# FFN accumulators in single PSUM banks, and the first pair's silu chain a few products later

## The chip, the cores and the metric

The kernel runs on one core of a Trainium2 chip. The metric is device time in microseconds of one launch; the time before is the median of three runs. One further execution was taken with the hardware profiler; its rows are what the prediction works with. Engines in those rows: PE (TensorE matmuls), PEld (TensorE weight loads), DVE (VectorE), ACT (ScalarE), POOL (GpSimd), SP (SyncE, which issues the DMAs).

## What is computed

One step of a two-layer streaming encoder over 640 rows (512 frames of a new stream, and 8 running streams of 16 frames) with a width of 1024, in fp32. Each layer is an FFN, a mixer, and another FFN; a last RMSNorm follows.

```python
for l in range(DEPTH):      # DEPTH = 2
    x = x + 0.5 * swiglu(rmsnorm(x, norm_g[l, 0]), ffn_w_gate[l, 0], ffn_w_up[l, 0], ffn_w_down[l, 0])
    hn = rmsnorm(x, norm_g[l, 1])
    out = mixer_ab(hn, ...) if l % 2 == 0 else mixer_c(hn, ...)
    x = x + out
    x = x + 0.5 * swiglu(rmsnorm(x, norm_g[l, 2]), ffn_w_gate[l, 1], ffn_w_up[l, 1], ffn_w_down[l, 1])

def swiglu(x, w_gate, w_up, w_down):
    return (jax.nn.silu(x @ w_gate) * (x @ w_up)) @ w_down
```

The inner width of an FFN is 2816. The mixers (mLSTM and SSD heads in layer 0, gated DeltaNet in layer 1) are untouched by the change except for the PSUM pool that they draw from.

## The kernel before

Activations lie transposed: eight tiles x of 128 features by 640 tokens. The stages run in order: FFN 0a, mixer ab, FFN 0b, FFN 1a, mixer gdn, FFN 1b; the last FFN ends in finish (L2065), which also writes the output. Every fp32 factor is split into a high and a low part, and each product is three matmul passes (high by high, high by low, low by high).

**PSUM.** A partition has eight banks of 512 fp32. One pool, opened in the constructor (L60), serves the whole program: big (L123) gives a tile of two banks, with two buffers, and small (L127) one bank, with four. The 640 tokens take two halves of 320 (HT), each in a bank of its own. A tile that is asked for when its tag's buffers are taken waits for the oldest one's readers.

**An FFN** (L653) works on 22 blocks of 128 inner columns, in eleven pairs, and builds one list of jobs that pipe (L589) issues. For each job: its matmuls, then sums for later weights on DVE, then the job's post (evictions), then the splits of weights that have become possible. in_order (L638) chains what a job issues to what the job before it issued on the same engine, so that PE, DVE, ACT and POOL each take the jobs in the order of the list.

- *Weights.* A unit of weights is split on ACT (high, L617) and POOL (low, L618) into two of eight buffers wsp, so a unit is split four units ahead, when the job of the unit four back is done. Raw weights come by DMAs of 1 MB (wload, L174).
- *The first pair* (first_jobs, L496) is done by plain products, since it runs while the block operands are still being made. Loop jobs 0 to 3 accumulate the gate's four sums (two big tiles) and half of up (q, two small), then rstd_cols (L359, one small); two jobs do the other half of up (v, two small), then rstd_rows (L372, into one big), which makes R, the per-token factor. end (L543) multiplies the gate by R, takes its silu on ACT, multiplies q and v by R out of PSUM, makes the last block operands (next(blocks): four L315 on ACT, four L316 on DVE) and the hidden activations (hidden, L478: L481 on DVE, L483 on ACT, L486 on DVE). loop_end (L521) copies the gate sums out of PSUM on ACT (L526) and makes the other block operands (blocks2, L309).
- *The other ten pairs* (pair_jobs, L430) use a scheme of seven block products in place of eight. The jobs of a pair are g4 (gate products 0 to 3), u4 (up 0 to 3), g3 (gate 4 to 6), u3 (up 4 to 6), each of twelve matmuls, then four down tiles of the group before. Product 0 to 3 open banks 0 to 3; products 4, 5 and 6 accumulate on banks 0, 2 and 3. The posts add the banks into an SBUF tile: product 0 is copied on ACT (p1, L456), the others are added on DVE (L452), and p4 ends with the gate's silu (L469). The gate's four banks are two big tiles, and up's four are small:

```python
if whole:
    x, y = self.big(), self.big()
    bank.update(enumerate((x[:, 0, :HT], x[:, 1, :HT], y[:, 0, :HT], y[:, 1, :HT])))
else:
    bank.update(enumerate(self.small()[:, :HT] for _ in range(4)))
```

- *Down* (down_jobs, L556): two of four down tiles are big and evicted by one DVE instruction, two are pairs of small and evicted by two (L580). In the first of the pair's groups a down tile has two blocks to sum over (12 matmuls), later four (24).
- *setup* (L146) for the coming mixer is called behind the first of the ten pairs in FFN 0a and 1a; its conv_setup (L904) takes three or six small tiles (L917) for short transposes, outside in_order.

At a stage's end each down tile is followed by prep (L298), which makes the next stage's operand xg from x. Each stage opens an SBUF pool of its own (section, L113) and closes it at its end.

Of the kernel before, what the change touches and what calls it, by code (L numbers as in the profile page):

```python
# [8 lines left out]
F32 = mybir.dt.float32  # L9
# [7 lines left out]
P = 128  # L17
T = 640
# [35 lines left out]
class Trunk:  # L54
    def __init__(self, ctx, tc, io):
# [3 lines left out]
        self.dram = ctx.enter_context(tc.tile_pool(name="dram", bufs=2, space=bass.MemoryType.DRAM))  # L59
        self.ps = ctx.enter_context(tc.tile_pool(name="ps", bufs=1, space=PSUM))  # L60
        self.n = 0
# [57 lines left out]
    def ext(self, which, dtype=F32):  # L119

        return lambda tag, shape, bufs=1: self.t(f"ext{which}", shape, {"A": 6, "B": 4, "C": 2}[which], dtype)

    def big(self):  # L123
        self.n += 1
        return self.ps.tile([P, 2, 512], F32, tag="big", name=f"big_{self.n}", bufs=2)

    def small(self):  # L127
        self.n += 1
        return self.ps.tile([P, 512], F32, tag="small", name=f"small_{self.n}", bufs=4)

# [299 lines left out]
    def pair_jobs(self, tile, raw, whole):  # L430
# [5 lines left out]
        def run(i, b, first, last):  # L436
            def go():
                if i == 0:
                    if whole:
                        x, y = self.big(), self.big()  # L440
                        bank.update(enumerate((x[:, 0, :HT], x[:, 1, :HT], y[:, 0, :HT], y[:, 1, :HT])))
                    else:
                        bank.update(enumerate(self.small()[:, :HT] for _ in range(4)))
                self.block_product(bank[b], w[i], [x[i] for x in self.xs], first, last)

            return go
# [49 lines left out]
    def first_jobs(self, tile, raw_g, raw_u, which, h):  # L496

        nc = self.nc
        blocks = self.blocks2(tile, which)
        G = [Unit(lambda m=m: raw_g.v[:, 2 * m : 2 * m + 2], None, raw_g if m == 3 else None, 2) for m in range(4)]  # L500
        Q, V = (
            [Unit(lambda m=m, c=c: raw_u.v[:, 4 * m : 4 * m + 4, c : c + P], None, raw_u if c and m else None) for m in range(2)] for c in (0, P)
        )
        ps, res = {}, {}

        def loop(m):
            def go():
                if m == 0:
                    ps["g"] = [self.big() for _ in range(2)]
                    ps["q"] = [self.small()[:, :HT] for _ in range(2)]  # L510
                for k in (2 * m, 2 * m + 1):
                    for c, t in enumerate(ps["g"]):
                        w = [part[:, k % 2, c * P : c * P + P] for part in G[m].parts]
                        self.half_passes([t[:, i, :HT] for i in range(2)], w, self.xg[k], k == 0, k == ND - 1)
                    self.half_passes(ps["q"], [part[:, k % 4] for part in Q[m // 2].parts], self.xg[k], k == 0, k == ND - 1)
                if m == 3:
                    self.rstd_cols()

            return go

        def loop_end(m):  # L521
            def go():
                if m == 3:
                    g, _ = res["g"], res["u"] = [tile("h", [P, 2 * T], bufs=8) for _ in range(2)]
                    for i, t in enumerate(ps["g"]):
                        nc.scalar.copy(g[:, i * T : i * T + T].rearrange("p (a b) -> p a b", a=2), t[:, :, :HT])  # L526
                next(blocks)

            return go

        def second(m):
            def go():
                if m == 0:
                    ps["v"] = [self.small()[:, :HT] for _ in range(2)]
                for k in range(4 * m, 4 * m + 4):
                    self.half_passes(ps["v"], [part[:, k % 4] for part in V[m].parts], self.xg[k], k == 0, k == ND - 1)
                if m == 1:
                    t = self.big()
                    self.rstd_rows(t[:, 0], t[:, 1])

            return go

        def end():  # L543
            g, u = res["g"], res["u"]
            for i in range(2):
                nc.vector.tensor_tensor(g[:, i * T : i * T + T], g[:, i * T : i * T + T], self.R, ALU.mult)
            nc.scalar.activation(out=g, in_=g, func=AF.Silu)
            for i, t in enumerate(ps["q"] + ps["v"]):
                nc.vector.tensor_tensor(u[:, i * HT : i * HT + HT], t, self.R[:, i % 2 * HT : i % 2 * HT + HT], ALU.mult)
            next(blocks)  # L550
            list(self.hidden(tile, g, u, h))

        jobs = [Job([G[m], Q[m // 2]], loop(m), loop_end(m)) for m in range(4)]
        return jobs + [Job([V[0]], second(0)), Job([V[1]], second(1), end)]

    def down_jobs(self, raw, h, j0, nxt):  # L556
# [6 lines left out]
        def job(j, c):  # L563
            unit, at, out, ps = units[c // b], c % b, [], []

            def run():
                if j % 4 < 2:
                    t = self.big()
                    ps.append(t[:, :, :HT])
                    out.extend(t[:, i, :HT] for i in range(2))  # L570
                else:
                    out.extend(self.small()[:, :HT] for _ in range(2))
                    ps.extend(out)
                for k in range(n):
                    self.half_passes(out, [part[:, k, at : at + P] for part in unit.parts], h[k], k == 0, k == n - 1)

            def post():
                x = self.x[j].rearrange("p (a b) -> p a b", a=2)
                for dst, src in [(x, ps[0])] if len(ps) == 1 else [(x[:, i], ps[i]) for i in range(2)]:
                    nc.vector.scalar_tensor_tensor(dst, src, 0.5, dst, ALU.mult, ALU.add)  # L580
                if nxt is not None:
                    nxt(j)
# [70 lines left out]
    def ffn(self, tile, l, s, nxt, mid):  # L653
# [23 lines left out]
        hs = [[] for _ in FF_GROUPS]  # L677
        jobs = self.first_jobs(tile, gates[0], ups[0], 3 * l + 2 * s, hs[0])
        for g, (g0, g1) in enumerate(FF_GROUPS):
            for f in range(max(g0, 2), g1, 2):  # L680
# [14 lines left out]
                u3[2].post = lambda post=u3[2].post, begin=begin: begin(post)  # L695
                down[0].post = lambda post=down[0].post, rest=rest: rest(post)
                jobs += g4 + u4 + g3 + u3 + down
                if f == 2 and mid is not None:
# [1366 lines left out]
    def finish(self, tile, w, acts):  # L2065
# [4 lines left out]
        for ts in (range(0, 3), range(3, NT)):  # L2070
# [48 lines left out]
    def run(self, stages):  # L2119
# [5 lines left out]

        self.load_x(0, 0, after(0))
        if stages[0][0] != "ffn":
            self.setup(stages[0][0])
# [57 lines left out]
```

## Time and profile before

| | us |
|---|---|
| median of three runs | 3109.37 |
| lowest, highest | 3107.22, 3112.12 |
| profiled execution | 3101.83 |
| its span, first to last instruction | 3100.1 |

| engine | busy us | share |
|---|---|---|
| PE | 2908.4 | 94% |
| PEld | 2766.8 | 89% |
| DVE | 1867.9 | 60% |
| POOL | 1459.7 | 47% |
| ACT | 1253.6 | 40% |

A row of the groups by shape reads: line, engine, operation, out<-in by the program's names, shapes, count, then busy us and mean ns of one, then the idle time of the engine just before those instructions and what ended it. A row of the timeline reads: start and length in us, engine, line, operation, out<-in, shapes, how many were merged, and in brackets the idle time before it and what ended that. big and small are the PSUM tags. Times are counted from the span's start. Where a wait is for several things, the view names the one that came last.

### The profile page before, as it was taken

What the parts mean: (1) busy time and instruction counts of PE and PEld (TensorE: products, weight loads), DVE (VectorE), ACT (ScalarE), POOL (GpSimd) and SP (SyncE); (2) the same over time, 40 slices, a digit from 0 to 9 for tenths busy, and PEclk for the clock granted to TensorE, in tenths of its full rate; (3) what the DMA queues carried; (4) which work ended last, traced back from release to release, by engine and by line L of the source; (5) the groups of instructions that cost most, each with busy time, mean ns of one, the idle gap of its engine ahead of it and who ended that gap; (6) DMA issues with size and microseconds to landing.
All of it is one profiled execution on the core that took longest, in us unless ns stands there. A gap on an engine that the chain in (4) does not pass through costs nothing. (4 is left out here: it accounts for less than half of the span.)

```text
span 3100.1 us, 51054 instructions
## 1 busy us (share of the span) xinstructions
PE 2908.4 (94%) x19910; PEld 2766.8 (89%) x19910; DVE 1867.9 (60%) x3455; ACT 1253.6 (40%) x2647; POOL 1459.7 (47%) x1039
## 2 busy tenths in 40 slices
PE   6999999999999998999998999999999998899998
PEld 6899999888889887999997999998888898899998
DVE  6565556323566676665655655556777756566665
ACT  5333334333344344333343333344565454333335
POOL 3666663222223125666644666653323222566664
PEclk8999999999999999999998999999999999999999
DMA  3222222222212221222221222221222212122222
GB/s 100 75 82 82 69 69 83 71 81 89 91 57 88 74 82 49 85 71 82 82 70 58 82 80 71 82 69 56 57 72 59 82 54 86 59 84 70 69 82 89
DMA packets 245159, 232.13 MB, mean 75 GB/s; under 512 B 22135, under 2 KB 221956, under 8 KB 244918
## 3 DMA queue, kind: packets, MB, share of 16 engines
q1 hardware_dynamic: 244918, 228.87, 23.9%
q8 instruction: 157, 2.57, 0.3%
q14 instruction: 84, 0.69, 0.1%
HBM read 210.23 MB, written 18.60 MB: 74 GB/s over the span
## 5 line engine op out<-in xcount | busy, mean ns | idle before, releaser
L618 POOL TENSOR_TENSOR wsp<-wraw,wsp 128x512 fp32r<-128x512 f32 x600 | 886.0, 1486 | 708.2 <-ACT wsp L617 679.8
L204 POOL TENSOR_TENSOR wsp<-wraw,wsp 128x512 fp32r<-128x512 f32 x216 | 292.5, 1361 | 796.3 <-ACT wsp L203 504.9
L617 ACT ACTIVATE wsp<-wraw 128x512 fp32r<-128x512 f32 x600 | 364.4, 626 | 396.1 <-PE big L421 166.3
L221 PE MATMUL big<-xg,wsp 128*128 128x320 f32 x2112 | 362.3, 319 | 0.0
L421 PE MATMUL big<-xg,wsp 128*128 128x320 f32 x1920 | 306.9, 312 | 38.7 <-ACT wsp L617 27.0
L221 PEld LDWEIGHTS big<-xg,wsp 128*128 128x128 f32 x2112 | 316.0, 190 | 20.9 <-issue 19.8
L421 PEld LDWEIGHTS big<-xg,wsp 128*128 128x128 f32 x1920 | 285.4, 188 | 50.0 <-ACT wsp L617 49.9
L492 PE MATMUL big<-h,wsp 128*128 128x320 f32 x2016 | 303.3, 309 | 0.0
L492 PE MATMUL small<-h,wsp 128*128 128x320 f32 x2016 | 303.2, 309 | 0.0
L492 PEld LDWEIGHTS big<-h,wsp 128*128 128x128 f32 x2016 | 297.7, 188 | 0.0
L492 PEld LDWEIGHTS small<-h,wsp 128*128 128x128 f32 x2016 | 297.6, 188 | 0.0
L421 PE MATMUL small<-xg,wsp 128*128 128x320 f32 x1920 | 294.3, 308 | 0.0
L421 PEld LDWEIGHTS small<-xg,wsp 128*128 128x128 f32 x1920 | 284.8, 188 | 0.0
L618 POOL TENSOR_TENSOR wsp<-S,wsp 128x512 fp32r<-128x512 f32 x160 | 237.9, 1498 | 84.6 <-ACT wsp L617 84.6
L767 PE MATMUL big<-wsp,xg 128*128 128x256 f32 x1920 | 244.5, 284 | 1.5 <-DVE zs L2061 1.4
L452 DVE TENSOR_TENSOR up<-small,up 128x320 f32<-128x320 f32 x200 | 97.8, 489 | 244.1 <-PE small L421 244.1
L452 DVE TENSOR_TENSOR gate<-big,gate 128x320 f32<-128x320 f32 x200 | 97.9, 490 | 241.2 <-PE big L421 241.2
L767 PEld LDWEIGHTS big<-wsp,xg 128*128 128x128 f32 x1920 | 233.2, 188 | 4.3 <-DVE zs L2061 2.1
L203 ACT ACTIVATE wsp<-wraw 128x512 fp32r<-128x512 f32 x216 | 136.0, 632 | 209.1 <-PE big L221 90.9
L421 PE MATMUL big<-extA,wsp 128*128 128x320 f32 x720 | 139.6, 331 | 77.7 <-ACT gate L456 54.3
L421 PEld LDWEIGHTS big<-extA,wsp 128*128 128x128 f32 x720 | 113.1, 197 | 99.0 <-ACT gate L456 65.0
L617 ACT ACTIVATE wsp<-S 128x512 fp32r<-128x512 f32 x160 | 99.2, 627 | 156.7 <-PE big L421 112.6
(486 smaller groups left out, 4827.4 us busy)
## 6 DMA issues: line engine op xcount, KB each, us to landing
wraw<-in_ffn_w_up SPq DMA_DIRECT2D x43, 1024.0 KB
wraw<-in_ffn_w_gate SPq DMA_DIRECT2D x43, 1024.0 KB
wraw<-in_ffn_w_down SPq DMA_DIRECT2D x38, 1024.0 KB
wraw<-in_ab_w_in SPq DMA_DIRECT2D x16, 1024.0 KB
wraw<-in_gdn_w_in SPq DMA_DIRECT2D x16, 1024.0 KB
wraw<-in_ffn_w_down SPq DMA_DIRECT2D x16, 512.0 KB
wraw<-in_ab_w_out SPq DMA_DIRECT2D x32, 256.0 KB
wraw<-in_ab_w_in SPq DMA_DIRECT2D x12, 512.0 KB
```

The source lines that it names most:

```text
L203: nc.scalar.activation(out=hi, in_=src[:, i : i + n], func=AF.Copy)
L204: nc.gpsimd.tensor_tensor(lo, src[:, i : i + n], hi.bitcast(F32), ALU.subtract)
L221: self.nc.tensor.matmul(ps[:, half, :HT], lhsT=wp, rhs=ap[:, half * HT : half * HT + HT], start=(k == 0 and i == 0), stop=(k == n - 1 and ...
L421: self.nc.tensor.matmul(ps, lhsT=unit.parts[wp][:, k], rhs=acts[k][:, ap], start=(first and k == 0 and i == 0), stop=(last and k == ND // ...
L452: nc.vector.tensor_tensor(c(dst), bank[b], c(src), ALU.add)
L492: self.nc.tensor.matmul(out[half], lhsT=wp, rhs=ap[:, half * HT : half * HT + HT], start=(first and i == 0), stop=(last and i == 2))
L617: nc.scalar.activation(out=u.parts[0], in_=src, func=AF.Copy)
L618: nc.gpsimd.tensor_tensor(u.parts[1], src, u.parts[0].bitcast(F32), ALU.subtract)
L767: self.nc.tensor.matmul(ps[:, t % 2, :256], lhsT=ap[:, t * P : (t + 1) * P], rhs=wp, start=(k == 0 and i == 0), stop=(k == ND - 1 and i == 2))
```

## The change

PSUM pools are opened by stage: banks(stack, n) opens one with n single banks and (8 - n) / 2 bank pairs. An FFN gets eight singles and no pair; the mixers, and the load of x ahead of the first stage, get four singles and two pairs as before. In the FFN's code every big becomes two small: the gate's four banks in pair_jobs, the four gate sums and the R rows in first_jobs, all down tiles (two DVE evictions each), and the product tile of finish (one single). loop_end copies the gate sums by four instructions in place of two.

The rest of end moves. What stays behind the first pair's last product is the multiplication of q and v by R, now first, and of the gate by R. The last block operands, the silu and hidden become a generator, rest, which is advanced once behind the post of each of the four g4 jobs of the next pair: operands and silu behind product 0, nothing behind product 1, L481 and L483 behind product 2, L486 behind product 3.

```diff
-        self.ps = ctx.enter_context(tc.tile_pool(name="ps", bufs=1, space=PSUM))
...
+    def banks(self, stack, n):
+
+        self.n += 1
+        self.ps, self.singles = stack.enter_context(self.tc.tile_pool(name=f"ps_{self.n}", bufs=1, space=PSUM)), n
+
     def big(self):
         self.n += 1
-        return self.ps.tile([P, 2, 512], F32, tag="big", name=f"big_{self.n}", bufs=2)
+        return self.ps.tile([P, 2, 512], F32, tag="big", name=f"big_{self.n}", bufs=(8 - self.singles) // 2)
 
     def small(self):
         self.n += 1
-        return self.ps.tile([P, 512], F32, tag="small", name=f"small_{self.n}", bufs=4)
+        return self.ps.tile([P, 512], F32, tag="small", name=f"small_{self.n}", bufs=self.singles)
...
                 if i == 0:
-                    if whole:
-                        x, y = self.big(), self.big()
-                        bank.update(enumerate((x[:, 0, :HT], x[:, 1, :HT], y[:, 0, :HT], y[:, 1, :HT])))
-                    else:
-                        bank.update(enumerate(self.small()[:, :HT] for _ in range(4)))
+                    bank.update(enumerate(self.small()[:, :HT] for _ in range(4)))
...
-                    ps["g"] = [self.big() for _ in range(2)]
+                    ps["g"] = [[self.small()[:, :HT] for _ in range(2)] for _ in range(2)]
...
-                    for i, t in enumerate(ps["g"]):
-                        nc.scalar.copy(g[:, i * T : i * T + T].rearrange("p (a b) -> p a b", a=2), t[:, :, :HT])
+                    for i, t in enumerate(ps["g"][0] + ps["g"][1]):
+                        nc.scalar.copy(g[:, i * HT : i * HT + HT], t)
...
-                    t = self.big()
-                    self.rstd_rows(t[:, 0], t[:, 1])
+                    self.rstd_rows(self.small(), self.small())
...
         def end():
             g, u = res["g"], res["u"]
+            for i, t in enumerate(ps["q"] + ps["v"]):
+                nc.vector.tensor_tensor(u[:, i * HT : i * HT + HT], t, self.R[:, i % 2 * HT : i % 2 * HT + HT], ALU.mult)
             for i in range(2):
                 nc.vector.tensor_tensor(g[:, i * T : i * T + T], g[:, i * T : i * T + T], self.R, ALU.mult)
-            nc.scalar.activation(out=g, in_=g, func=AF.Silu)
-            for i, t in enumerate(ps["q"] + ps["v"]):
-                nc.vector.tensor_tensor(u[:, i * HT : i * HT + HT], t, self.R[:, i % 2 * HT : i % 2 * HT + HT], ALU.mult)
+
+        def rest():
             next(blocks)
-            list(self.hidden(tile, g, u, h))
+            nc.scalar.activation(out=res["g"], in_=res["g"], func=AF.Silu)
+            yield
+            yield
+            yield from self.hidden(tile, res["g"], res["u"], h)
...
             def run():
-                if j % 4 < 2:
-                    t = self.big()
-                    ps.append(t[:, :, :HT])
-                    out.extend(t[:, i, :HT] for i in range(2))
-                else:
-                    out.extend(self.small()[:, :HT] for _ in range(2))
-                    ps.extend(out)
+                out.extend(self.small()[:, :HT] for _ in range(2))
...
-                for dst, src in [(x, ps[0])] if len(ps) == 1 else [(x[:, i], ps[i]) for i in range(2)]:
-                    nc.vector.scalar_tensor_tensor(dst, src, 0.5, dst, ALU.mult, ALU.add)
+                for i in range(2):
+                    nc.vector.scalar_tensor_tensor(x[:, i], out[i], 0.5, x[:, i], ALU.mult, ALU.add)
...
-        jobs = self.first_jobs(tile, gates[0], ups[0], 3 * l + 2 * s, hs[0])
+        jobs, beside = self.first_jobs(tile, gates[0], ups[0], 3 * l + 2 * s, hs[0])
...
+                if f == 2:
+                    for job in g4:
+                        job.post = lambda post=job.post: (post(), next(beside))
                 jobs += g4 + u4 + g3 + u3 + down
...
-                    ps = self.big()[:, 0, :m]
+                    ps = self.small()[:, :m]
...
-        self.load_x(0, 0, after(0))
+        with ExitStack() as section:
+            self.banks(section, 4)
+            self.load_x(0, 0, after(0))
...
                 tile = self.section(section, kind)
+                self.banks(section, 8 if kind == "ffn" else 4)
```

More of the change, by code (lines that the diff above doesn't have):

```diff
@@ L513, in go @@
                         w = [part[:, k % 2, c * P : c * P + P] for part in G[m].parts]
-                        self.half_passes([t[:, i, :HT] for i in range(2)], w, self.xg[k], k == 0, k == ND - 1)
+                        self.half_passes(t, w, self.xg[k], k == 0, k == ND - 1)
                     self.half_passes(ps["q"], [part[:, k % 4] for part in Q[m // 2].parts], self.xg[k], k == 0, k == ND - 1)
@@ L544, in end @@
             g, u = res["g"], res["u"]
+            for i, t in enumerate(ps["q"] + ps["v"]):
+                nc.vector.tensor_tensor(u[:, i * HT : i * HT + HT], t, self.R[:, i % 2 * HT : i % 2 * HT + HT], ALU.mult)
             for i in range(2):
                 nc.vector.tensor_tensor(g[:, i * T : i * T + T], g[:, i * T : i * T + T], self.R, ALU.mult)
-            nc.scalar.activation(out=g, in_=g, func=AF.Silu)
-            for i, t in enumerate(ps["q"] + ps["v"]):
-                nc.vector.tensor_tensor(u[:, i * HT : i * HT + HT], t, self.R[:, i % 2 * HT : i % 2 * HT + HT], ALU.mult)
+        def rest():
             next(blocks)
-            list(self.hidden(tile, g, u, h))
+            nc.scalar.activation(out=res["g"], in_=res["g"], func=AF.Silu)
+            yield
+            yield
+            yield from self.hidden(tile, res["g"], res["u"], h)
         jobs = [Job([G[m], Q[m // 2]], loop(m), loop_end(m)) for m in range(4)]
-        return jobs + [Job([V[0]], second(0)), Job([V[1]], second(1), end)]
+        return jobs + [Job([V[0]], second(0)), Job([V[1]], second(1), end)], rest()
     def down_jobs(self, raw, h, j0, nxt):
@@ L563, in job @@
         def job(j, c):
-            unit, at, out, ps = units[c // b], c % b, [], []
+            unit, at, out = units[c // b], c % b, []
             def run():
-                if j % 4 < 2:
-                    t = self.big()
-                    ps.append(t[:, :, :HT])
-                    out.extend(t[:, i, :HT] for i in range(2))
-                else:
-                    out.extend(self.small()[:, :HT] for _ in range(2))
-                    ps.extend(out)
+                out.extend(self.small()[:, :HT] for _ in range(2))
                 for k in range(n):
@@ L2124, in after @@
             return lambda d, total=True: self.prep(d, 3 * l + {"a": 0, "b": 2}.get(s, 1), total)
-        self.load_x(0, 0, after(0))
-        if stages[0][0] != "ffn":
-            self.setup(stages[0][0])
+        with ExitStack() as section:
+            self.banks(section, 4)
+            self.load_x(0, 0, after(0))
+            if stages[0][0] != "ffn":
+                self.setup(stages[0][0])
         for i, (kind, l, s) in enumerate(stages):
```

## Prediction

> **What bounds it now.** I read the waits by total first, then the groups of instructions by shape, then the timeline of one pair of feed-forward columns late in the program, and the busy time of that pair by engine.
>
> The waits view (engine, line waited before, what ended the wait: us in total, times, longest):
>
> ```profile
> PE big L421 <- ACT gate L456: 54.3, 40, 9.1
> ...
> PE big L421 <- ACT wsp L617: 27.0, 40, 0.7
> ...
> PE big L421 <- DVE gate L452: 23.4, 40, 0.6
> ...
> PE big L421 <- DVE x L580: 11.7, 8, 1.5
> ```
>
> Forty is the number of pairs that go through the seven block products: ten in each of four FFNs. So three kinds of wait come once in every pair, all on tiles named big, the two-bank ones. The groups by shape show the same products where they write single banks:
>
> ```profile
> L421 PE MATMUL small<-xg,wsp 128*128 128x320 f32 x1920 | 294.3, 308 | 0.0
> ...
> L421 PE MATMUL small<-extA,wsp 128*128 128x320 f32 x720 | 125.1, 309 | 0.0
> ```
>
> The up columns run the same plan with the same evictions, on four singles, and the idle time before their matmuls is 0.0. The timeline of one pair, and its row of busy times (length, PE, PEld, DVE, ACT, POOL, granted clock):
>
> ```profile
> 2764.26 1.93 PE L421 MATMUL big<-xg,wsp 128*128 128x320 f32 x12
> ...
> 2766.70 1.14 PE L421 MATMUL big<-extA,wsp 128*128 128x320 f32 x6 [0.51 <-ACT gate L456]
> ...
> 2771.08 1.14 PE L421 MATMUL big<-extA,wsp 128*128 128x320 f32 x6 [0.58 <-DVE gate L452]
> ...
> 2783.59 0.63 ACT L617 ACTIVATE wsp<-wraw 128x512 fp32r<-128x512 f32 x1 [1.14 <-PE big L421]
> 2783.68 0.49 DVE L452 TENSOR_TENSOR gate<-big,gate 128x320 f32<-128x320 f32 x1 [1.27 <-PE big L421]
> ...
> 2784.32 2.01 PE L421 MATMUL big<-xg,wsp 128*128 128x320 f32 x12 [0.67 <-ACT wsp L617]
> ...
> 2791.45 7.20 PE L492 MATMUL big<-h,wsp 128*128 128x320 f32 x48
> 2798.49 7.20 PE L492 MATMUL small<-h,wsp 128*128 128x320 f32 x48
> ```
>
> ```profile
> 2764.43:2805.69 41.26, 39.49 (x266) 38.72 (x266) 25.09 (x32) 13.90 (x23) 26.47 (x19) 1.00 0.24 77
> ```
>
> TensorE is the bound: DVE, ACT and POOL have 14 us or more to spare in the pair. Undisturbed, 48 matmuls take 2798.49 - 2791.45 = 7.04 us, 0.1467 us each. A pair has 7 + 7 products of 12 matmuls and four down tiles of 24, 264 in all, 38.73 us; it takes 41.26. The missing 2.53 us are the three stalls (0.51 + 0.58 + 0.67 idle) and the slower first matmul behind each. In the first, product 1 writes the second bank of a pair while ACT copies product 0 out of the first; in the second, product 3 stands to product 2 in the same way. For the third the view names ACT L617, but that splits a later unit's weights, already four ahead; DVE L452, which reads product 5 in the other half of product 6's tile, ended at 2784.17, within 0.05 us of it, and up, which has the same L617, never waits there. I take all three for one cause: two tiles' worth of work sharing one tile.
>
> **The steady pairs.** With eight singles no product shares a tile with one that is being read. Sixteen tiles are taken per pair, twice round the ring, so gate and up fill it once and the four down tiles once; each tile comes back a half pair or more after its reader, so no new wait follows. I cost the three waits at nothing afterwards. What hides the evictions is the other seven banks; what is late next is the weights' split, four units ahead (5.3 us) and needing 0.63 on ACT plus about 1.5 on POOL (below). 36 pairs (all but the one behind each first pair) x 2.53 = 91.1 us. The third stall's share by idle time is 0.67 / 1.76 x 2.53 = 0.96; in the other four pairs, 3.9 us.
>
> Down tiles are read by two instructions in place of one:
>
> ```profile
> L618 POOL TENSOR_TENSOR wsp<-wraw,wsp 128x512 fp32r<-128x512 f32 x600 | 886.0, 1486 | 708.2 <-ACT wsp L617 679.8 <-DVE extC L316 23.6
> ...
> L580 DVE SCALAR_TENSOR_TENSOR x<-small,x 128x320 f32<-128x320 f32 x184 | 80.7, 478 | 19.6 <-PE small L492 19.1
> ...
> L580 DVE SCALAR_TENSOR_TENSOR x<-big,x 128x640 f32<-128x640 f32 x92 | 74.0, 816 | 11.3 <-PE big L492 11.3
> ```
>
> 2 x 478 - 816 = 140 ns, 92 times: 12.9 us of DVE, in a pair where DVE idles 16 us. On the path: 0; if that cover were gone, 12.9.
>
> **The first pair and the products behind it.** This is the part with moved work. The last FFN, in order of time:
>
> ```profile
> 2640.53 2.01 PE L421 MATMUL big<-xg,wsp 128*128 128x320 f32 x12
> ...
> 2642.21 0.69 DVE L405 TENSOR_TENSOR S<-S,wraw 128x512 f32<-128x512 f32 x1
> 2642.82 1.55 DVE L546 TENSOR_TENSOR h<-h,R 128x640 f32<-128x640 f32 x2
> 2644.28 1.68 DVE L549 TENSOR_TENSOR h<-small,R 128x320 f32<-128x320 f32 x4
> 2644.40 1.27 ACT L547 ACTIVATE h<-h 128x1280 f32<-128x1280 f32 x1 [1.30 <-DVE h L546]
> 2645.58 1.53 ACT L315 ACTIVATE xg<-h 128x320 fp32r<-128x320 f32 x4
> 2646.07 1.70 DVE L316 TENSOR_TENSOR xg<-h,xg 128x320 fp32r<-128x320 f32 x4
> 2647.68 1.48 DVE L481 TENSOR_TENSOR h<-h,h 128x1280 f32<-128x1280 f32 x1
> 2649.20 1.27 ACT L483 ACTIVATE h<-h 128x1280 fp32r<-128x1280 f32 x1 [2.09 <-DVE h L481]
> ...
> 2651.35 1.97 PE L421 MATMUL big<-extA,wsp 128*128 128x320 f32 x6 [8.81 <-ACT gate L456]
> ...
> 2651.91 1.77 DVE L408 TENSOR_TENSOR wraw<-wraw 128x512 f32<-128x512 f32 x1
> ...
> 2666.85 3.68 PE L421 MATMUL big<-xg,wsp 128*128 128x320 f32 x24
> ```
>
> Product 1 waits 8.81 us, because ACT's copy of product 0 is queued behind the silu, the four L315 and L483. It then starts cold (six matmuls in 1.97 us). The eight products of g4 and u4 take 2666.85 - 2640.53 = 26.3 us; at full pace 96 x 0.1467 = 14.1.
>
> Afterwards, on the same clock. DVE is free of the sums at 2642.90; q and v come first (four of 0.42, to 2644.6), then L546 (to 2646.1), L316 (1.70, to 2647.9), L408 (0.7 to 1.77; I take 1.0) and two adds of 0.49 (to 2649.9), L481 (to 2651.4). Taking tiles in ring order, product 0 gets the fourth bank (a gate sum already copied), and product 1 the first q bank: it waits for the first q multiplication, 2643.4, 1.1 us after product 0. Products 1 to 3 then run on, to 2648.75. ACT: copy of product 0, four L315, silu once L546 is done (2646.1 to 2647.4), then the split of the weights of u4's first product, ready on POOL at 2649.6: the third matmul needs it at 2649.05, so +0.6. ACT's L483 now waits for L481 to 2651.4, ends at 2652.7, and queued behind it is the split for u4's third product, on POOL to 2655.0, while that product would start at 2652.9: about 2.0 us. Sum 1.1 + 0.6 + 2.0 = 3.7 over 14.1: 17.8 in place of 26.3, a gain of 8.5 x 4 = 34 us. Ends: 12.2 each if nothing of the moved chain shows, 6 each if those stalls bring the half clock again. I take 8.5, from the rows.
>
> What does not go: nine tiles live where rstd is taken.
>
> ```profile
> 2629.45 1.26 ACT L526 COPY h<-big 128x640 f32<-128x640 f32 x2
> ...
> 2629.76 9.90 PE L492 MATMUL small<-xg,wsp 128*128 128x320 f32 x47 [2.18 <-DVE rstd L365]
> ```
>
> v's second tile then takes the first gate bank, whose copy (half as long, four in place of two) ends at about 2629.9: the same wait, 0.15 us later, 4 x 0.15 = 0.6 lost.
>
> Behind the next pair's short down tiles the gate waits for DVE's L580; and in two FFNs setup's transposes take three and six tiles of the same ring ahead of it:
>
> ```profile
> 1694.61 1.12 PE L421 MATMUL big<-xg,wsp 128*128 128x320 f32 x6 [1.47 <-DVE x L580]
> ...
> 1698.25 0.87 DVE L580 SCALAR_TENSOR_TENSOR x<-small,x 128x320 f32<-128x320 f32 x2
> ```
>
> Half a tile is free 0.34 us sooner (816 - 478): 6 x 0.34 = 2.0 gained. With six setup tiles the gate's first tile falls on the last down tile, read at 1698.25 + 0.44: 4.1 us late; with three, about 1.0: 5.1 lost (0 if tiles are given out as they are first written). The last stage takes its product tiles from the ring too, eight deep in place of two: I take 0.
>
> **The stage boundaries.** PSUM now changes pools at six of them. What a new pool waits for is not in the trace for PSUM; for SBUF it is:
>
> ```profile
> 502.34 4.24 PE L792 MATMUL big<-xg,wsp 128*64 128x320 f32 x28
> ...
> 505.09 0.88 DVE L580 SCALAR_TENSOR_TENSOR x<-small,x 128x320 f32<-128x320 f32 x2
> ```
>
> ```profile
> 1605.12 10.00 SPq L177 DMA_DIRECT2D wraw<-in_ffn_w_up  x2
> ...
> 1614.56 1.92 PE L492 MATMUL big<-xg,wsp 128*128 128x320 f32 x12
> ...
> 1617.02 0.88 DVE L580 SCALAR_TENSOR_TENSOR x<-small,x 128x320 f32<-128x320 f32 x2
> ...
> 2604.00 1.55 DVE L743 TENSOR_TENSOR x<-big,x 128x640 f32<-128x640 f32 x2
> ```
>
> The second of those two loads, into the new FFN's own pool, goes out at the end of the 10 us, when the old FFN's last product is done, though the slot's own reader ended some 42 us (twelve down tiles) before: a pool waits for all of the old one. For PSUM that means all of the last L580. FFN to FFN: 1617.9 - 1614.56 = 3.4 us of idle TensorE. FFN to mixer, twice: 506.0 - 502.34 = 3.6, less 0.7 that L792 already loses later: 2.9 each. The other three already follow an eviction that is the last but one, as at 2604.00, where the FFN waits for the first L743 of two: half of 1.55, 0.8 each. Sum 11.6. Idle of 2.18 us above was followed by 47 matmuls in 9.90 us, 3.0 more than at full pace, so I add 2.5 for each of the three long drains: 19.1. Ends: 0 (tile by tile) and 22.
>
> The Trainium skill, "TensorE: Matmul & The Clock Gate", section "What's actually happening", has the clock fall to half only after an idle window of about 3.4 us. By that rule drains of 3.4 to 3.6 us would mostly miss it, and the boundaries would cost 11.6. The row with 2.18 us disagrees, and I go by the row.
>
> **Sum.** 91.1 + 3.9 + 34 + 2.0 - 0.6 - 5.1 - 19.1 = 106.2 us. The profiled execution took 3101.83 us (a span of 3100.1 and 1.7 around it) and would become 2996. It lies 7.5 us, 0.24%, under the median of the three runs, 3109.37; on the scale of the medians that is 3003.
>
> **Rivals.** *No drains*: PSUM tiles wait bank by bank. For it: tiles within a pool do. Against: the load above. 3003 - 19 = 2984.
> *Drains at full clock*: the idle at the boundaries does not bring the half clock: 3003 - 7.5 = 2996. For it: 1.47 us of idle before 1694.61 was followed by six matmuls in 1.12 us, full pace; against: the 2.18 us row. This is also what the Trainium skill's rule above would make of it.
> *The third stall is ACT's*, as the view names it, and stays: 40 x 0.96 = 38 us, 3041. Against: up's zero idle.
> *The first pair's queue is worse*: L483 holds back the splits long enough to bring the half clock in all four FFNs, and setup's tiles do too: 4 x 2.5 + 10 = 20, 3023.
> *It does not do what it says*: the waits come from elsewhere than the shared tile, and all three stay. Then only 34 less 24 is gained: 3099. Against: 2640 matmuls on singles without idle.
> *Slower*: POOL becomes the bound. TensorE now asks for 18 splits in 38.7 us rather than 41.26. Place: the fourteen products of each pair. It decides where a split takes more than 41.26 / 18 = 2.29 us on average; at 2.5 us a pair takes 45.0, 40 x 3.74 = 150 us more, less the 34, with 24 for boundaries and setup: about 3250. Against: a mean of 1486 ns, 26.47 us of a pair.
>
> **Numbers.** The forecast 0.50, own range 2980 to 3025; drains at full clock 0.16, no drains 0.10, third stall 0.08, queue 0.07, nothing removed 0.04, POOL 0.03, and 0.02 for losses that just cancel the gain. About 0.2%, 6 us, is what a measurement of this kernel can tell from no change: the first six lie beyond it on the fast side, so faster 0.95, same 0.02, slower 0.03. The range runs from all unknown costs at their good ends (19 + 5 + 14 more: 2965, cut to 2972) to just past the third stall's case, 3044.
>
> **What would show it.** Right: idle before L421 0.0 on every tile but the first products behind the first pair; a steady pair at about 38.8 us; product 1 behind the first pair about 1 us late instead of 8.8, and a wait on wsp at u4's third product; 3 to 4 us of idle TensorE at 0b to 1a and before L792, ended by L580. Wrong: an L617 wait that stays at product 6; a POOL wait in every pair; no gap at the boundaries.

## The result, and the profile after

The change is faster: 3029.59 us (median; 3028.85 to 3035.38) against 3110.74 (3107.22 to 3113.76) measured beside it, a ratio of 0.9744 (95% interval 0.9727 to 0.976). The forecast was 3003 with a range of 2972 to 3044: the sign and the range held, 81 us came of the 106 forecast. The forecast's own narrower range, 2980 to 3025, did not hold. The profiled execution after took 3035.38 us, 5.8 above its median, and the one before 3101.83, 8.9 below the median of 3110.74, so the two traces lie closer together (66.4 us by their spans) than the medians do.

The stages, from the view that sums stretches (start and end, length, busy time of PE, PEld, DVE, ACT and POOL with the number of instructions, granted clock, DMA share, GB/s): mixer gdn, FFN 1b and finish. Before:

```profile
2094.57:2604.96 510.39, 483.95 (x3680) 446.04 (x3678) 358.84 (x998) 271.39 (x768) 152.79 (x131) 0.97 0.23 66
2604.96:3053.13 448.17, 417.04 (x2756) 408.74 (x2757) 270.31 (x376) 159.38 (x258) 269.51 (x184) 0.98 0.23 72
3053.13:3100.12 46.99, 35.86 (x244) 33.01 (x242) 28.69 (x75) 29.00 (x71) 16.86 (x13) 0.93 0.32 113
```

After:

```profile
2020.46:2546.62 526.16, 500.84 (x3678) 461.47 (x3679) 355.60 (x994) 269.99 (x766) 151.15 (x129) 0.94 0.22 63
2546.62:2962.13 415.51, 408.80 (x2756) 407.45 (x2757) 269.04 (x395) 158.51 (x259) 273.92 (x183) 0.99 0.25 78
2962.13:3033.66 71.53, 37.45 (x244) 32.93 (x242) 32.43 (x75) 31.25 (x71) 16.52 (x13) 0.96 0.21 74
```

The four FFNs together went from 1884.3 to 1766.3 us, 118 saved. Three things gave 51.6 back: finish 24.5 (46.99 to 71.53), the mixers 25.2 (ab 638.7 to 648.1, gdn 510.4 to 526.2), the load of x 1.9. Note the PE column of finish: the busy time hardly grew, the idle time did. In gdn it is the other way round: PE is busy 16.9 us longer with the same instructions, and the granted clock (the share of full speed that TensorE is allowed) is lower.

The waits after (engine, line waited before, what ended it: us in total, times, longest us):

```profile
PE small L2095 <- ACT tmp L2091: 26.1, 16, 2.1
PE small L425 <- ACT wsp L614: 8.5, 4, 2.6
PE small L425 <- DVE x L577: 8.5, 6, 2.2
...
PE small L425 <- POOL wsp L615: 4.1, 6, 1.0
...
PE big L792 <- DVE v L1259: 3.6, 1, 3.6
PE big L792 <- DVE x L577: 3.5, 1, 3.5
...
PE small L492 <- ACT h L329: 3.0, 1, 3.0
```

All three rows with a count of forty are gone. (L425 is the matmul of a block product, L421 before; splits are L614 and L615, the down eviction L577.) A new row leads: sixteen waits of L2095, the transposes of finish. The eight products behind the first pair, and one steady pair:

```profile
2577.38:2597.91 20.53, 17.29 (x100) 16.63 (x99) 18.08 (x23) 10.69 (x18) 14.25 (x10) 0.83 0.01 1
2768.60:2807.30 38.70, 38.70 (x266) 38.70 (x265) 25.08 (x34) 13.91 (x23) 26.87 (x19) 1.00 0.26 83
```

The steady pair runs without a gap: 38.70, length and PE busy alike, where it was 41.26 and 39.49.

### The profile page after: what moved, and what is told of

It reads as the page before. It is cut to its first block, busy times and chain, and to the rows that moved or that the text cites. A ratio compares the mean times of both kernels' runs of the same rounds, so it can differ in the third digit from the quotient of the medians.

```text
span 3033.7 us, 51436 instructions
## 1 busy us (share of the span) xinstructions
PE 2901.8 (96%) x19910; PEld 2784.1 (92%) x19910; DVE 1884.2 (62%) x3547; ACT 1255.1 (41%) x2655; POOL 1474.1 (49%) x1039
## 5 line engine op out<-in xcount | busy, mean ns | idle before, releaser
L615 POOL TENSOR_TENSOR wsp<-wraw,wsp 128x512 fp32r<-128x512 f32 x600 | 887.0, 1489 | 608.2 <-ACT wsp L614 561.3
L425 PE MATMUL small<-xg,wsp 128*128 128x320 f32 x3840 | 593.3, 312 | 20.3 <-ACT wsp L614 8.5
L492 PE MATMUL small<-h,wsp 128*128 128x320 f32 x4032 | 597.9, 309 | 0.0
L425 PEld LDWEIGHTS small<-xg,wsp 128*128 128x128 f32 x3840 | 575.0, 190 | 24.2 <-ACT wsp L614 19.5
L492 PEld LDWEIGHTS small<-h,wsp 128*128 128x128 f32 x4032 | 593.1, 188 | 0.0
L614 ACT ACTIVATE wsp<-wraw 128x512 fp32r<-128x512 f32 x600 | 364.4, 626 | 361.5 <-PE small L425 218.5
L225 PE MATMUL big<-xg,wsp 128*128 128x320 f32 x2112 | 370.2, 323 | 0.0
L225 PEld LDWEIGHTS big<-xg,wsp 128*128 128x128 f32 x2112 | 323.2, 194 | 21.8 <-issue 20.7
L615 POOL TENSOR_TENSOR wsp<-S,wsp 128x512 fp32r<-128x512 f32 x160 | 253.6, 1597 | 47.0 <-ACT wsp L614 36.0
L425 PE MATMUL small<-extA,wsp 128*128 128x320 f32 x1440 | 253.9, 312 | 1.0 <-POOL wsp L615 0.9
L425 PEld LDWEIGHTS small<-extA,wsp 128*128 128x128 f32 x1440 | 224.2, 190 | 2.0 <-POOL wsp L615 2.0
L425 PE MATMUL small<-extB,wsp 128*128 128x320 f32 x960 | 180.3, 310 | 0.0
L577 DVE SCALAR_TENSOR_TENSOR x<-small,x 128x320 f32<-128x320 f32 x368 | 157.7, 479 | 29.9 <-PE small L492 29.1
L483 ACT ACTIVATE h<-up 128x1280 fp32r<-128x1280 f32 x40 | 51.0, 1275 | 266.1 <-DVE up L481 266.1
L425 PEld LDWEIGHTS small<-extB,wsp 128*128 128x128 f32 x960 | 151.5, 189 | 0.0
L614 ACT ACTIVATE wsp<-S 128x512 fp32r<-128x512 f32 x160 | 99.1, 627 | 110.7 <-PE small L425 60.5
```

Of the source, the lines that this page charges most:

```text
L225: self.nc.tensor.matmul(ps[:, half, :HT], lhsT=wp, rhs=ap[:, half * HT : half * HT + HT], start=(k == 0 and i == 0), stop=(k == n - 1 and ...
L425: self.nc.tensor.matmul(ps, lhsT=unit.parts[wp][:, k], rhs=acts[k][:, ap], start=(first and k == 0 and i == 0), stop=(last and k == ND // ...
L483: nc.scalar.activation(out=hi, in_=u, func=AF.Copy)
L492: self.nc.tensor.matmul(out[half], lhsT=wp, rhs=ap[:, half * HT : half * HT + HT], start=(first and i == 0), stop=(last and i == 2))
L577: nc.vector.scalar_tensor_tensor(x[:, i], out[i], 0.5, x[:, i], ALU.mult, ALU.add)
L614: nc.scalar.activation(out=u.parts[0], in_=src, func=AF.Copy)
```

## The experiments

Ratios are to the kernel before, run on the same chip; the change itself has 0.9744. "Region" is the time of the eight products behind the first pair, in FFN 0a, 0b, 1a and 1b: 26.2, 25.8, 25.8, 26.3 before; 18.1, 20.5, 20.0, 20.5 after.

### Where finish lost its time

Before, product tiles of finish were big and transpose tiles small. After, both are small, in one rotation. Two ways to undo that, first with pools (ring holds the PSUM pool that is open):

```diff
...
         if nxt is None:
+            self.ring.close()
+            self.banks(self.ring, 4)
             self.finish(tile, wd[:, FF_GROUPS[-1][0] :], hs[-1])
...
-                    ps = self.small()[:, :m]
+                    ps = self.big()[:, 0, :m]
```

> The kernel after, but the rotation of eight is closed ahead of the finish, which gets the PSUM pool of the kernel before (two pairs for its products, four singles for its transposes). Theory (the finish lost 24.5 us, 46.99 to 71.53, because products and transposes draw from one tag and TensorE can no longer run product j+1 between a product and its transposes): the waits of about 1.7 us ended by ACT L2091 go, the finish is 47 to 50 us again, with one more drain of 1 to 3 us at its start; the whole is 20 to 24 us below the kernel after (3029.6), so 3006 to 3010. Rival (the finish is long for another cause that came with the change: weights that land later, or a lower clock): within 5 us of the kernel after, and the waits stay.

Measured: 3006.88 us, ratio 0.9679 (0.9661 to 0.9697); finish 48.5 us. The second keeps the rotation and changes only the order in which the tiles are asked for (turn holds the transposes and their two kinds of copies):

```diff
...
+                    if late is not None:
+                        turn(*late)
+                    late = j, xf
+            turn(*late)
...
```

> The kernel after with its one rotation kept in the finish; only the program order is changed: the transposes of tile j and their copies are written behind product j+1. Theory (order of the tiles handed out, not the number of banks or pools): the finish falls by 20 to 25 us to about 47 to 51, the whole to 3005 to 3010. Rival (a pool of pairs is needed, because a bank of the rotation comes free too late): waits on earlier evictions take the place of those on ACT L2091, gain under 8 us. Rival (weights or clock): no change.

Measured: 3002.82 us, 2 us below the expected range, ratio 0.9671 (0.9654 to 0.9688); finish 49.0 us. The start of finish on PE, before, after, and here (transposes are L2095, L2095 and L2080; products L2081, L2081 and L2092):

```profile
3053.13 4.15 PE L2081 MATMUL big<-h,wsp 128*128 128x384 f32 x23
3057.12 0.52 PE L2095 MATMUL small<-ident,tmp 128*128 128x128 f32 x3
3057.39 2.51 PE L2081 MATMUL big<-h,wsp 128*128 128x384 f32 x13
```

```profile
2962.13 2.24 PE L2081 MATMUL small<-h,wsp 128*128 128x384 f32 x12
2966.09 0.55 PE L2095 MATMUL small<-ident,tmp 128*128 128x128 f32 x3 [1.71 <-ACT tmp L2091]
2966.39 2.34 PE L2081 MATMUL small<-h,wsp 128*128 128x384 f32 x12
2970.44 0.55 PE L2095 MATMUL small<-ident,tmp 128*128 128x128 f32 x3 [1.71 <-ACT tmp L2091]
```

```profile
2951.24 4.33 PE L2092 MATMUL small<-h,wsp 128*128 128x384 f32 x24
2955.41 0.49 PE L2080 MATMUL small<-ident,tmp 128*128 128x128 f32 x3
2955.65 2.33 PE L2092 MATMUL small<-h,wsp 128*128 128x384 f32 x12
```

Before, two products (23 records) run ahead of the first transposes: product 1 covers the eviction, square and scaling of tile 0. After, twelve, then a wait, sixteen times. The source writes the transposes of tile j ahead of product j + 1 in both kernels, but finish lies outside in_order, so with two tags the product could go first. With one tag it could not: the transposes of tile j draw their bank ahead of product j + 1. With the program order turned the same eight banks do nearly as well as the two tags did (49.0 us against 47.0). The rivals (weights, clock, a bank too few) are out. In size this is the distance between the forecast and the result, some 24 us; that the rest agrees so well is in part luck (below).

### Which tile the third stall was

The kernel before, with the gate's four sums dealt crosswise over its two pairs:

```diff
-                        bank.update(enumerate((x[:, 0, :HT], x[:, 1, :HT], y[:, 0, :HT], y[:, 1, :HT])))
+                        bank.update(enumerate((x[:, 0, :HT], y[:, 0, :HT], x[:, 1, :HT], y[:, 1, :HT])))
```

> The kernel before, gates only: the gate's two pairs are dealt crosswise, sums 0 and 2 in one, 1 and 3 in the other. In the order of the products 0,1,2,3,0,2,3 one product is then left (the second use of sum 2) that writes the tile whose other bank the step before it is still read from. Theory of the shared tile: two of the three stalls per pair go and one stands at that product, ended by DVE: of 2.53 us a pair some 0.8 stay, gain 57 to 66 us, 3045 to 3054. Rival (the stalls are those of the rotation as a whole): gain under 20; and if the third stall was ACT's, it stays where it was (in front of sum 3), not at sum 2.

Measured: 3042.61 us, ratio 0.9797 (0.9778 to 0.9816), by that 63 us faster. The last three products of a gate are sums 0, 2 and 3 again. In the kernel before, two of them ran together (24 matmuls) and the third waited (2784.32, shown in the prediction):

```profile
2779.97 3.68 PE L421 MATMUL big<-xg,wsp 128*128 128x320 f32 x24
```

Here one runs (12) and the second waits; the steady pair's length is below:

```profile
2890.82 1.92 PE L421 MATMUL big<-xg,wsp 128*128 128x320 f32 x12
2893.41 3.76 PE L421 MATMUL big<-xg,wsp 128*128 128x320 f32 x24 [0.68 <-ACT wsp L617]
```

```profile
2837.13:2876.75 39.62, 38.95 (x266) 38.71 (x265) 23.39 (x32) 13.92 (x23) 26.95 (x19) 1.00 0.25 80
```

The stall moved with the tile, to the product whose bank neighbour is still being read, while the splits stayed where they were; the view still names ACT L617. So the name was wrong and the prediction's reading right. What the name shows is only which of several things waited for came last in the trace.

The next deals both columns so that no neighbour is ever read: sums 1 and 3 in a pair, 0 and 2 in singles.

```diff
-                    if whole:
-                        x, y = self.big(), self.big()
...
+                    x, y, z = self.big(), self.small(), self.small()
+                    bank.update(enumerate((y[:, :HT], x[:, 0, :HT], z[:, :HT], x[:, 1, :HT])))
```

> The kernel before with its own one pool (two pairs, four singles) for the whole program; only the hand-out in a pair's products is changed: gate and up each take one pair for sums 1 and 3 and two singles for sums 0 and 2, so that no product writes a tile whose other bank the step before it still has to read. Theory (all three stalls per pair are a shared tile: TensorE waits for the reader of the other bank): the 36 steady pairs lose 2.53 us each and the other four about 1, gain 91 to 97, nothing lost in the finish, at the boundaries or in the mixers, so 3011 to 3022. Rival (the third stall is ACT's and not the tile's): 57 us, 3054. Rival (what helped is that all eight banks rotate freely): gain under 30.

Measured: 3035.36 us, ratio 0.9778 (0.9755 to 0.98); a miss, 13 us above the expected range. In gain it is a larger one, about 68 us for the 91 to 97 expected, since the kernel before ran at 3102.88 us beside it. A steady pair is 39.03 us, so the stalls are gone as expected and without any pool change. With the moved chain on top:

> The kernel before with the hand-out of pairs_1_3 and the moved chain of the change, still in its one pool. Theory (both parts add, and the pools of the change only cost): 3110.7 - 95 - 25 = 2990, range 2980 to 3000, and the mixers stay at their lengths of before (638.7 and 510.4). Rival (the mixers grew by 25 us in the kernel after because the clock gives back what the FFNs gain): mixers near 648 and 526, the whole 3010 to 3020.

Measured: 3023.28 us, ratio 0.9738 (0.9714 to 0.9761), a miss, 23 us above the range. The waits of the two:

```profile
PE small L421 <- DVE h L546: 17.0, 4, 4.4
```

```profile
PE small L421 <- DVE h L543: 13.5, 4, 4.0
```

Sums 0 and 2 of the gate now need singles, and behind the first pair all four are held by q and v until DVE has scaled them: the very first product waits 2.7 to 4.4 us per FFN. The FFNs together fell by 80.2 and 95.2 us, against 118.0 in the change. That is a cost of my hand-out, and shows what the change's eight free banks are for. The rest of the miss is in the mixers, and is not the pools', which are the old ones here (below).

### What the moved chain is worth

The change without the moved chain (end as before), and the kernel before with it alone:

```diff
...
-        def rest():
-            next(blocks)
...
+            next(blocks)
+            list(self.hidden(tile, g, u, h))
...
```

> The kernel after with its one rotation of eight banks, but the first pair's chain (gate scaling, silu, q and v scaling, last block parts, hidden halves) back in one go behind the last product of the first pair. Theory (the moved chain brought the whole gain of the first-pair region, 26.0 to 19.8 us on the mean of four FFNs): 4 x 6.2 = 25 us above the kernel after, so 3055, range 3048 to 3062, and the steady pairs stay as in the kernel after. Rival (the region gained because the gate tiles no longer share banks in pairs, and the move is worth nothing): within 6 us of 3030.

> The kernel before with only the first pair's chain moved as in the change; pools and hand-out as before. Theory (the move is worth 6 us per FFN by itself): 3110.7 - 25 = 3086, range 3078 to 3094. Rival (with bank pairs the first pair's products meet the tiles of the next pair, and the move only shifts the wait): within 6 us of the kernel before.

Measured: chain_back 3037.24 us, ratio 0.9774 (0.9757 to 0.9791); chain_only 3083.11 us, 0.9926 (0.9904 to 0.9948). On the old banks the move is worth 0.74%, 23 us, near the 25 expected; in the traces the FFNs fall by 30.3. In the change it is worth 0.3%, 9 us, with intervals that overlap; by the traces' FFNs 15.2. The first stated theory (25) and the rival (nothing) both miss. The wait ahead of gate product 3 in chain_back, FFN 1b, and ACT before it:

```profile
2586.63 0.90 PE L425 MATMUL small<-extA,wsp 128*128 128x320 f32 x2 [6.50 <-ACT wsp L610]
```

```profile
2580.00 1.27 ACT L546 ACTIVATE h<-h 128x1280 f32<-128x1280 f32 x1 [3.55 <-DVE h L545]
2581.17 1.53 ACT L319 ACTIVATE xg<-h 128x320 fp32r<-128x320 f32 x4
2584.79 1.27 ACT L483 ACTIVATE h<-h 128x1280 fp32r<-128x1280 f32 x1 [2.08 <-DVE h L481]
2585.97 0.61 ACT L610 ACTIVATE wsp<-wraw 128x512 fp32r<-128x512 f32 x1
```

With eight banks the products run on over the chain until the weights that are split ahead are used up: 6.5 us of wait, where the bank pairs made it 8.8 at product 1. So the two parts of the change buy partly the same microseconds. Regions: chain_back 22.4, 25.1, 25.3, 25.4; chain_only 17.6, 21.9, 19.1, 21.3.

### The 2.6 us that are left behind the first pair

After the change, FFN 1b, DVE, ACT and PE:

```profile
2580.56 1.77 DVE L409 TENSOR_TENSOR S<-S,wraw 128x512 f32<-128x512 f32 x1 [1.19 <-POOL wsp L615]
2582.26 1.67 DVE L545 TENSOR_TENSOR h<-small,R 128x320 f32<-128x320 f32 x4
2583.85 1.55 DVE L547 TENSOR_TENSOR h<-h,R 128x640 f32<-128x640 f32 x2
```

```profile
2585.43 1.27 ACT L551 ACTIVATE h<-h 128x1280 f32<-128x1280 f32 x1 [2.83 <-DVE h L547]
2586.61 0.61 ACT L614 ACTIVATE wsp<-wraw 128x512 fp32r<-128x512 f32 x1
```

```profile
2587.28 0.90 PE L425 MATMUL small<-xg,wsp 128*128 128x320 f32 x2 [2.62 <-ACT wsp L614]
```

DVE is done with the scaling 8.0 us after the first product's start (2585.40 - 2577.38) where I had reckoned 5.6, since a weight sum (L409) stands ahead and waits for POOL; the silu waits for that, and the split for u product 0 waits behind the silu. I moved the silu away, on top of finish_late_turn: one product later, three products later with the hidden steps behind u products 0 and 1, and three later with the hidden steps later still (the diff shows this last one).

```diff
...
             next(blocks)
-            nc.scalar.activation(out=res["g"], in_=res["g"], func=AF.Silu)
             yield
+            nc.scalar.activation(out=res["g"], in_=res["g"], func=AF.Silu)
             yield
...
-                    for job in g4:
+                    for job in (g4[0], g4[3], g3[1], g3[2]):
```

> finish_late_turn with the first pair's silu issued one product later than in the change. Theory (the silu blocks whichever split stands behind it until about 8 us after the first product's start): the wait moves from u product 0 to u product 1, which is due 2.1 us later, so some 1 us is left: gain about 2 us per FFN, 5 to 10 us below 3002.8. Rival (the split is late for another cause): no change.

> finish_late_turn with the first pair's silu issued behind the fourth of the next products instead of the first, and the two hidden steps behind the next pair's u products 0 and 1. Theory (in the kernel after the first u product waits 2.6 us for ACT's split and 0.6 us for POOL's because that split stands behind a silu that has to wait for DVE's scaling): the waits on ACT L614 and POOL L615 in the first pair's region go, 3.2 us in three FFNs and some 2 in 0a, with up to 3.4 us of half clock behind each; 9 to 20 us below finish_late_turn (3002.8), so 2983 to 2994. Rival (the split itself is late, because of weights or DVE's weight sums): the waits stay, within 4 us of 3003.

> finish_late_turn with the first pair's chain spread wider: last block parts behind gate product 0, silu behind gate product 3, the two hidden steps behind the third part's gate products (sums 2 and 3 again). In silu_fourth the wait had moved: none at u product 0 any more, but 2.4 us for ACT's split and 1.6 us for POOL's at the first product behind the u products, where ACT's split stood behind the hidden copy L483 that waited for DVE L481. Theory (only the steps of the chain that wait for DVE hold the splits up, so that behind the fuller rotation they hold up nothing): those 4 us go as well, 2 to 4 us per FFN below finish_late_turn, 2987 to 2996. Rival (DVE itself is full there, its scalings, block parts, weight sums and stores of the sums are some 19 us without a gap, and whatever is put behind it waits): the wait moves once more, within 4 us of 3003.

Measured: 3010.55 us, 0.9682 (0.9667 to 0.9696); 3005.89, 0.9672 (0.9658 to 0.9686); 3001.89, 0.9664 (0.9644 to 0.9685). None can be told from finish_late_turn's 0.9671. So the theories' gains did not come, and the rivals were nearer in time; the waits did not stay, though, they moved. In silu_fourth u product 0 waits no longer, the product behind the u products does:

```profile
2598.98 0.56 PE L425 MATMUL small<-xg,wsp 128*128 128x320 f32 x2 [2.44 <-ACT wsp L616]
2601.11 5.17 PE L425 MATMUL small<-xg,wsp 128*128 128x320 f32 x18 [1.57 <-POOL wsp L617]
```

In chain_spread the regions are down to 15.4 to 15.8 us, 62.8 in sum where finish_late_turn has 80.0; but of these 17 us some 14 are lost again before the same pair ends, and the four FFNs together are no shorter (1763.6 against 1761.8 us). In FFN 1b a wait of 1.58 us for POOL comes further on. What may have a part in it, though no run separates it: with the splits going out earlier, POOL works while DVE scales, and DVE slows down. The same two L547 that took 1.55 us above, and POOL beside them, in chain_spread:

```profile
2578.61 3.42 DVE L547 TENSOR_TENSOR h<-h,R 128x640 f32<-128x640 f32 x2
```

```profile
2578.23 3.12 POOL L615 TENSOR_TENSOR wsp<-S,wsp 128x512 fp32r<-128x512 f32 x2
```

### The boundaries

One PSUM pool for FFN 0b and 1a together, once on the change, once on silu_fourth:

```diff
...
-                self.banks(section, 8 if kind == "ffn" else 4)
+                if i != 3:
+                    stack = pair if i == 2 else section
+                    self.banks(stack, 8 if kind == "ffn" else 4)
```

> The kernel after, but FFN 0b and FFN 1a, which follow each other, share one PSUM pool of eight, so that no pool ends between them. Theory (the 3.02 us of idle TensorE at that boundary is the drain of the pool): the idle time falls under 1 us, gain 2 to 4 us. Rival (the boundary waits on the normalised input of the next FFN, as the trace's releaser, ACT h L329, says): no change within 1 us. The other boundaries and the finish stay as in the kernel after.

> silu_fourth, and one PSUM pool of eight for FFN 0b and FFN 1a together, as in one_pool_0b_1a (3024.5 against 3029.6, not surely different). Theory (the end of the pool between them drains TensorE for 2 to 3 us): 2 to 5 us below silu_fourth. Rival (the boundary waits for DVE's last sums and the next input anyway): within 1.5 us of silu_fourth. Gaps of TensorE at the boundary tell it whatever the times.

Measured: 3024.53 us, 0.974 (0.972 to 0.9759), and 3009.18, 0.968 (0.9666 to 0.9693): no difference that the times can tell. PE at the boundary does tell it, after and with one pool:

```profile
1561.78 3.39 PE L492 MATMUL small<-h,wsp 128*128 128x320 f32 x22
1568.19 6.98 PE L492 MATMUL small<-xg,wsp 128*128 128x320 f32 x46 [3.02 <-ACT h L329]
```

```profile
1557.73 6.47 PE L492 MATMUL small<-h,wsp 128*128 128x320 f32 x43
1564.03 8.23 PE L492 MATMUL small<-xg,wsp 128*128 128x320 f32 x55
```

The gap of 3.02 is the drain of the pool, the wait for its last readers, although the view names ACT. Without the pool's end there is none. The time gain that was expected in silu_fourth_one_pool, 2 to 5 us, cannot be seen.

### The mixers

The mixers' code is the same in all these kernels, but not their time. Gdn took 526.2 us after and 512.9 in chain_back, which have the same pools, and 523.1 in pairs_1_3, which has the old pool and no drain:

```profile
2031.09:2544.02 512.93, 486.61 (x3679) 448.30 (x3679) 356.51 (x994) 269.93 (x766) 150.97 (x129) 0.97 0.23 64
```

```profile
2043.61:2566.70 523.09, 498.03 (x3680) 458.65 (x3678) 358.65 (x997) 269.93 (x766) 151.62 (x130) 0.94 0.23 64
```

Length goes with the granted clock. In the trace's record of the clock, half speed (half clock, for short) comes in stretches of 3.413 us and its multiples, all on one grid, and the grid stands elsewhere against the program in each execution (its offset from the span's start, modulo 3.413, was 0.79 before, 3.11 after, 0.56 in chain_back). Gdn had 27.3 us of half clock before, 64.8 after, 34.1 in chain_back, 58.0 in pairs_1_3; less half of that, the four lengths are 496.8, 493.8, 495.9 and 494.1. So the difference in length is half clock, and short and long stages occur with either kind of pool.

Whether the pools have a part in it stays open. Gdn took 523.9 to 526.2 us in seven of the nine traces with pools by stage, and over 516 in only one of the five with the old pool. But in those seven it began 0.1 to 0.8 us behind a line of the grid, and in none of the other seven did it: the two causes fall together here. How the grid fell would fit the distance between 66 us by the traces and 81 by the medians, since the trace before has a short gdn and the trace after a long one.

## Why the prediction was right in kind and 25 us too high in size

- *Shared tile, three stalls, 91.1 us.* Right, cause and size: a pair went from 41.26 to 38.70, 36 x 2.56 = 92.2. The third stall was the tile's (pairs_0_2). The Trainium skill, "PSUM — Partial Sum Buffer", section "Summary: rules for kernel authors", says that reading PSUM while a matmul runs needs only a different bank. The traces agree as far as they go: once the neighbours were tiles of their own nothing waited, so the wait lay in the tile that spanned two banks.
- *First pair, 34 us.* Too high: the regions fell by 25.0 in sum. Product 1 did not wait for a q bank at all, so free banks cannot have been handed out in the order of the ring; instead u product 0 waited 2.6 + 0.6 us, where I had 0.6, because DVE's wait for POOL ahead of L545 had been left out, and half clock followed (0.83 over the region). The 2.0 us at u4's third product did not come.
- *v1's wait, -0.6.* Wrong sign: the waits before v1 went from 9.5 us in sum to 3.5, and the half clock in the four first pairs from 20.5 us to 6.8. From an FFN's first matmul to its first block product, the four together went from 143.5 to 130.6 us, 12.9 shorter. Why the wait is gone or nearly so in three FFNs stays open.
- *The small terms, 3.9, 2.0 and -5.1.* About right: from the end of the eight products to the start of the third pair behind the first, the four FFNs went from 231.4 to 222.6 us, 8.8 less, where these terms and the stalls of four pairs make 10.9. Setup's tiles cost 4.9 us in FFN 1a and 0.8 in 0a.
- *Boundaries, -19.1 with half clock.* Nearly right: the drains came, 3.57, 3.02 and 3.51 us, with TensorE starting 0.15 us behind the end of the last L577 each time, whatever the view names, and at the other three boundaries 0.73, 0.73 and 1.85 more than before: 13.4 against 11.6. Half clock came with two of the three long ones, so the rival of drains at full clock holds at one. The rival without drains is out.
- *"The last stage takes its product tiles from the ring too, eight deep in place of two: I take 0."* This is the step that failed, and the one that carries the miss. I counted banks and not the order in which one tag hands them out: sixteen waits, 26.1 us, finish 24.5 longer. Put right alone, it gives 3002.8 to 3006.9, against the 3003 forecast. That close a fit is luck: the 9.0 us too much for the products behind the first pair and the 13.5 too little for the first pair itself cancel in part, and the mixers' time, which the sum did not have, is half clock that came or did not.

No rival of the prediction had the finish in it, and the result lies inside the whole range only because that reached to the third stall's case, which did not happen. The balance by the traces: 118.0 - 24.5 - 25.2 - 1.9 = 66.4 us. Of the expectations, chain_back's missed because I held the moved chain's gain to be independent of the banks, those of pairs_1_3 and pairs_1_3_chain because I held the half-dealt pairs to be free of side effects, and the gains of the three silu runs and of silu_fourth_one_pool did not come.

The best kernels here are finish_late_turn, 3002.82 us, and chain_spread, 3001.89, about 0.8% below the change; they cannot be told apart.

## What to carry to other kernels

Merging two tags of tiles into one rotation gives more banks and takes away a freedom: products and the short steps between them then take banks in program order, so turn the program order (the short step behind the next product) wherever the two tags had let them overlap, in the stages that the change was not about as well. Two tiles' worth of work in one tile serialises a writer with its neighbour's reader; dealing the pair to steps that are never adjacent is a test of that, and a fix that needs no new pool, if the single banks it asks for are free (here they were not, behind each first pair). When a wait sits behind a queue, list every wait ahead on that queue and on the engine that feeds it: moving the step that is last only moves the wait if the feeder is full.

## What the runs showed of the hardware

Half clock does not need 3.4 us of idle time. In five traces (before, after, chain_back, finish_late_turn, pairs_1_3) no interval of the 3.413 us grid at full speed with more than 1.86 us of idle TensorE was left without half clock behind it (64 had more); in the other nine two were, with 1.89 us (silu_fourth_one_pool) and 1.94 (pairs_0_2), and none with more. The gap of 3.02 us at 1568.19, after the change, fell with 1.24 and 1.78 us on two intervals and brought none. Some intervals with less idle time were followed too; what else counts is open. The Trainium skill, "TensorE: Matmul & The Clock Gate", section "What's actually happening", has a free-running window of 3413 ns, which the records agree with, and one idle window as the condition, which they do not.

DVE's L547, with two inputs in SBUF, took 0.81 us each in all eight cases after the change, with no POOL instruction beside it, and 1.54 to 1.93 in all sixteen of silu_fourth and chain_spread, with POOL's splits beside it. The Trainium skill, "SBUF — State Buffer", section "Who interferes with whom", says that two such inputs contend with a GpSimd instruction that reads SBUF; the rows agree, and 0.7 to 1.1 us per instruction is what it cost here.
